# Order of table reads and weight loads in the state-space stage of a two-layer decoder trunk

## The chip, the cores and the metric

The kernel runs on one core of a Trainium2 chip. The metric is device time in microseconds (us) of one execution; the figure given is the median of the runs. Engines are called by their short names in the profile: PE is the matrix engine (TensorE), ACT is ScalarE, DVE is VectorE, POOL is GpSimd and SP is SyncE. All numbers are float32.

## The reference

Two layers work on a sequence of 512 tokens with 1024 channels. Layer 0 mixes tokens with a grouped complex state-space model (S5), layer 1 with attention; each is followed by a gated feed-forward part with a short convolution. Before each of the four parts there is an RMS norm, modulated by a shift and a scale that come from a conditioning vector c; the result is gated by a third vector of the same origin and added to the residual.

```python
def adaln_params(c, w, b):
    mod = jax.nn.silu(c) @ w + b
    shift, scale, gate = jnp.split(mod, 3, axis=-1)

def s5_mixer(h, w_in, ...):
    u = h @ w_in
    # 64 groups of 16 channels; each group drives 64 complex states:
    # x[t] = lb * x[t-1] + bb @ u[t];   y[t] = Re(c @ x[t])
    y = y + d_skip * u
    y = jax.nn.gelu(y)
    y = y * jax.nn.sigmoid(y @ w_glu)
    return y @ w_out
```

The change lies in the S5 part alone.

## The kernel before

The S5 part works on eight blocks of 128 channels (eight groups each). Tokens are cut into 64 places of 8 tokens. For one block m the work is:

1. **Projection.** u[m] = x @ w_in[m]: eight matmuls (`project`, L1270), evicted by ACT to the tile `uf` and written by SP to a DRAM scratch `s_ud` (`projected`, L1275 and L1276). SP reads it back in another layout, channel and token along the partitions (`read_u`, L1280; tile `u`). The read waits for the write to land.
2. **Kernel table.** Small matmuls (`s5_inputs`, L1032) make `w1` and the tile `kt`. DVE adds the skip weights `dd` to `kt`, and SP writes it to a DRAM scratch `s_z` (`s5_kernel`, L1047 and L1050). SP then reads it back as a Toeplitz table `tw`, 512 KB in rows of 512 bytes that overlap in DRAM (`s5_toeplitz`, L1057). The read waits for the write to land. ACT masks the table to `t` (`s5_masked`, L1066).
3. **States.** PE forms the state inputs of each place from `u` and `w1` (`s5_blocks`, L1090); DVE rotates, scans and rotates back (`s5_scan`, from L1106).
4. **Outputs.** PE adds what comes from the inputs of the place, `t` times `u` (`s5_from_inputs`, L1131), and what comes from the states (`s5_from_states`, L1142). ACT applies gelu, SP writes the result to scratch `s_yd` (`s5_gelu`, L1155 and L1156) and reads it back as `h` (L1159).

The loop `for m in range(KT - 2)` (L1347) pipelines this by hand. Round m runs the states and outputs of block m, the kernel table of block m+1 and the projection of block m+2. All engines run in the order in which the program is written (`manual_schedule`), and each engine takes its instructions, DMA issues among them, strictly in that order: an instruction that waits holds up all behind it on the same engine.

Two queues issue transfers here. SP issues the scratch writes and reads named above. POOL issues the loads from the inputs, since `self.loads` is set to POOL at L1318: the projection matrices `w_in` (`load_w`, 512 KB each, "raw<-in_s_w_in"), the skip weights (`load_d`, 64 KB each, "dd<-in_s_dd") and the modulation matrices ("raw<-in_ada_w", 512 KB each). These last belong to two generators: `ada` makes the gate of the S5 part out of eight matrices, and `ada2` shift and scale of the next part out of sixteen. Each `next(...)` of them runs the matmuls of two matrices (L226) and issues two further loads; the first `next` only issues four loads. A load waits until a slot of its tile is free: the tag `raw` has three slots, `w_hi` and `w_lo` five each.

Before the loop POOL carries out two small additions into a tile `gate`, whose value is used nowhere. The first (L1317) reads a parameter; the second (L1341) reads the first kernel table, so that the POOL instructions behind it are not issued until that table has landed. Behind it come the first four loads of `ada`. In round 0, POOL then issues the fourth projection matrix and the third skip weights (L1349 and L1350), and after round 0's outputs the last four loads of `ada`. SP reads in round 0 first the third u (L1368) and then the second kernel table (L1369).

## Time and profile before

| what | value |
|---|---|
| median of 3 runs | 1211.98 us (1211.89 to 1212.69) |
| profiled execution, its own time | 1213.4 us |
| its span, first to last instruction | 1211.6 us |
| mean granted PE clock | 0.992 |
| PE busy | 1178.7 us, 97% of the span |
| DVE busy | 1008.2 us, 83% |
| ACT busy | 614.7 us, 51% |
| POOL busy | 120.6 us, 10% |
| DMA moved | 182.00 MB, mean 150 GB/s |

Times in the rows are us from the start of the span. A row of a timeline has the start, the length, engine, source line, operation, output tile, input tile and count, and in square brackets how long the engine was idle before it and what ended that idle time. A row that starts a DMA on SP or POOL shows its issue; when the data landed is told by the DMA view, as us from issue to landing. Queue q1 carries what SP issues and q0 what POOL issues.

### The profile page before, as it was taken

The page shows a single profiled execution, that of the slowest core. Times are in us where ns is not written, and L with a number is a line of the kernel's source. Part 1 is how long each engine was busy: PE and PEld are TensorE (multiplying, and loading weights), DVE is VectorE, ACT ScalarE, POOL GpSimd, SP SyncE. Part 2 cuts the span into 40 slices and gives each one's busy share as a digit, 9 for nine tenths or more (in the row PEclk, how much of TensorE's full clock was granted, in tenths as well). Part 3 has the DMA queues.
Part 4 walks back from the last instruction along what each step waited for, and adds up shares of the span by engine and source line. Part 5 has one row for each costly group of instructions (what it writes and reads, how often), then busy time and mean ns, then how long its engine had stood idle before and what let it go on. Part 6 is the DMA issues. An engine that isn't in the chain of part 4 may idle for free.

```text
span 1211.6 us, 20653 instructions
## 1 busy us (share of the span) xinstructions
PE 1178.7 (97%) x7925; PEld 1019.7 (84%) x7925; DVE 1008.2 (83%) x1843; ACT 614.7 (51%) x1179; POOL 120.6 (10%) x227
## 2 busy tenths in 40 slices
PE   7979999999999999999999999999999999999997
PEld 2555678898989889999899888878989999999987
DVE  8967896879999999898698578876899888888865
ACT  3625563436445455555443566664366545545553
POOL 3211111100000000000000334430000000000000
PEclk9989999999999999999999999999999999999999
DMA  9596767832355555433445443432223332323331
GB/s 369 174 344 199 243 205 260 278 115 67 111 178 166 169 162 166 149 111 103 126 139 194 168 164 127 148 118 90 77 64 103 121 110 93 106 99 109 109 101 70
DMA packets 71826, 182.00 MB, mean 150 GB/s; under 512 B 23103, under 2 KB 24479, under 8 KB 70703
## 3 DMA queue, kind: packets, MB, share of 16 engines
q1 hardware_dynamic: 58767, 137.94, 35.2%
q0 software_dynamic: 11632, 41.95, 10.2%
q8 instruction: 62, 1.02, 0.3%
q10 hardware_dynamic: 1328, 0.79, 0.2%
q14 instruction: 37, 0.30, 0.1%
HBM read 173.73 MB, written 6.92 MB: 149 GB/s over the span
## 4 chain that ended last, share of the span: by engine, by line
PE 56%; issue 17%; DVE 6%; DMA 4%; ACT 1%; POOL 1%; SPq 0%; DVEq 0%; POOLq 0%; ACTq 0%
PE mmp L317 27%; PE mmp L586 16%; PE aux L586 6%; PE mmp L1594 2%; DVE w_lo L301 2%; PE aux L1733 1%; DMA raw<-in_s_w_out 1%; PE aux L1753 1%; DVE ada_raw L270 1%; PE aux L1703 1%; DMA ada_raw<-in_ada_t 1%; POOL ada_raw L256 1%; ACT w_hi L300 1%; DMA nf<-nfd 1%; DMA raw<-in_w_down 1%
## 5 line engine op out<-in xcount | busy, mean ns | idle before, releaser
L301 DVE TENSOR_TENSOR w_lo<-raw,w_hi 128x1024 fp32r<-128x1024 f32 (+4 forms) x173 | 182.8, 1061 | 26.7 <-ACT w_hi L300 26.2
L300 ACT ACTIVATE w_hi<-raw 128x1024 fp32r<-128x1024 f32 (+4 forms) x173 | 153.8, 899 | 89.6 <-PE mmp L317 34.5
L317 PE MATMUL mmp<-ghi,w_lo 128*128 128x512 f32 (+1 forms) x412 | 147.5, 358 | 1.1 <-DVE w_lo L301 1.1
L317 PE MATMUL mmp<-ghi,w_hi 128*128 128x512 f32 (+1 forms) x412 | 147.9, 359 | 0.3 <-DVE h L399 0.3
L317 PE MATMUL mmp<-glo,w_hi 128*128 128x512 f32 (+1 forms) x412 | 147.4, 358 | 0.0
L586 PE MATMUL mmp<-w_hi 128*128 128x256 f32 x420 | 116.6, 278 | 1.7 <-ACT nm_h L593 1.1
L317 PE MATMUL mmp<-a_hi,w_hi 128*128 128x512 f32 (+1 forms) x320 | 116.7, 368 | 1.5 <-ACT a_hi L469 1.5
L586 PE MATMUL mmp<-w_lo,w_hi 128*128 128x256 f32 x420 | 116.2, 277 | 0.0
L586 PE MATMUL mmp<-w_hi,w_lo 128*128 128x256 f32 x420 | 116.0, 277 | 0.0
L317 PE MATMUL mmp<-a_hi,w_lo 128*128 128x512 f32 (+1 forms) x320 | 114.4, 358 | 0.0
L317 PE MATMUL mmp<-a_lo,w_hi 128*128 128x512 f32 (+1 forms) x320 | 114.2, 358 | 0.0
L301 DVE TENSOR_TENSOR w_lo<-sums,w_hi 128x1024 fp32r<-128x1024 f32 x78 | 94.8, 1218 | 0.0
L300 ACT ACTIVATE w_hi<-sums 128x1024 fp32r<-128x1024 f32 x78 | 81.0, 1054 | 25.9 <-DVE sums L554 22.4
L593 ACT ACTIVATE nm_h<-mmp 128x256 f32<-128x256 f32 x105 | 39.3, 380 | 100.7 <-PE mmp L586 100.5
L317 PEld LDWEIGHTS mmp<-ghi,w_lo 128*128 128x128 f32 x412 | 77.4, 188 | 13.4 <-DVE w_lo L301 1.9
L317 PEld LDWEIGHTS mmp<-ghi,w_hi 128*128 128x128 f32 x412 | 77.4, 188 | 11.2 <-issue 0.4
L317 PEld LDWEIGHTS mmp<-glo,w_hi 128*128 128x128 f32 x412 | 77.4, 188 | 10.2
L586 PEld LDWEIGHTS mmp<-w_hi 128*128 128x128 f32 x420 | 78.9, 188 | 2.6 <-ACT nm_h L593 1.5
L586 PE MATMUL mmp<-a_hi,w_lo 128*128 128x256 f32 x280 | 77.8, 278 | 1.3 <-DVE w_lo L301 1.1
L586 PEld LDWEIGHTS mmp<-w_hi,w_lo 128*128 128x128 f32 x420 | 78.7, 188 | 0.2 <-DVE w_lo L301 0.2
L586 PEld LDWEIGHTS mmp<-w_lo,w_hi 128*128 128x128 f32 x420 | 78.9, 188 | 0.0
L586 PE MATMUL mmp<-a_hi,w_hi 128*128 128x256 f32 x280 | 77.9, 278 | 0.2 <-ACT w_hi L300 0.2
(335 smaller groups left out, 3123.3 us busy)
## 6 DMA issues: line engine op xcount, KB each, us to landing
raw<-in_w_up SPq DMA_DIRECT2D x88, 512.0 KB, 3.8
ada_raw<-in_ada_t POOLq DMA_DIRECT2D x40, 512.0 KB, 4.1
raw<-in_ada_w POOLq DMA_DIRECT2D x24, 512.0 KB, 6.2
nf<-nfd SPq DMA_DIRECT2D x8, 1152.0 KB, 6.5
raw<-in_ada_w SPq DMA_DIRECT2D x16, 512.0 KB, 9.9
raw<-in_fox_qk SPq DMA_DIRECT2D x16, 512.0 KB, 3.5
raw<-in_w_down SPq DMA_DIRECT2D x24, 320.0 KB, 3.0
rawd<-in_w_down SPq DMA_DIRECT2D x24, 256.0 KB, 3.2
```

Of the source, the lines that this page charges most:

```text
L256: (nc.gpsimd if late else nc.sync).dma_start(ws[n], src)
L270: nc.vector.tensor_tensor_reduce(w, w, self.c_row, 1.0, 0.0, ALU.mult, ALU.add, sums[:, j:j + 1])
L300: self.rounded = nc.scalar.activation(hi, src, AF.Copy).ins
L301: return nc.vector.tensor_tensor(lo, src, hi.bitcast(F32), ALU.subtract)
L317: self.last_mm = self.nc.tensor.matmul(o if len(xt.shape) == 2 else by_place(o), wt, xt, start=(k == 0 and n == 0), stop=(k == nk - 1 and ...
L586: self.last_mm = nc.tensor.matmul(o, wt[:, k], xt[:, k], start=(first and k == 0 and n == 0), stop=(k == H - 1 and n == 2), skip_group_che ...
L593: a = nc.scalar.activation(t, o, AF.Copy)
L1594: self.last_mm = nc.tensor.matmul(ps[q, b][:, :n], xt[:, k, tb], wt, start=(k == 0 and i == 0), stop=(k == KT - 1 and i == 2),)
L1703: nc.tensor.matmul(ps[b][r], q[i][a, tq], kk[j][a, :N], start=(n == 0), stop=(n == 2), tile_position=(64 * r, 0), skip_group_check=True,)
L1733: nc.tensor.transpose(pt[:, r - rs[0], k, :], s[:, r, k * P:(k + 1) * P], self.ident)
L1753: nc.tensor.matmul(pv[:, c * P:], self.v[:, hp, k, r].rearrange("p t d -> p (t d)"), pp[:, r, c + 3 * k:NB + 3 * k, :].rearrange("p b t -> ...
```

## The change

Three things are done, all in the S5 part:

- The fourth projection matrix (`load_w(3)`) and the third skip weights (`load_d(2)`) are issued by POOL ahead of the loop, right behind the second skip weights and ahead of the gate on the first kernel table, instead of in round 0. The rounds from 1 on are as before.
- In round 0, SP's read of the second kernel table (`s5_toeplitz(1)`) stands ahead of its read of the third u (`read_u(2)`). In the other rounds the order is as before.
- In round 0, POOL carries out one more addition into `gate`, which reads the second kernel table. Behind it in POOL's order come the last four loads of `ada` and all that POOL issues from round 1 on.

```diff
@@ -1319,6 +1319,8 @@
                 load_d(0)
                 load_w(2)
                 load_d(1)
+                load_w(3)
+                load_d(2)
                 read_u(0)
                 turns = self.s5_rotations(0)
                 next(turns)
@@ -1345,9 +1347,10 @@
                 turns = self.s5_rotations(2)
                 next(turns)
                 for m in range(KT - 2):
-                    if m + 3 < KT:
+                    if m and m + 3 < KT:
                         load_w(m + 3)
-                    load_d(m + 2)
+                    if m:
+                        load_d(m + 2)
                     ps = self.s5_blocks(ws[m], us[m])
                     if m:
                         self.s5_gelu(m - 1, yps.pop(m - 1))
@@ -1364,9 +1367,10 @@
                     if m:
                         next(turns)
                         t = self.s5_masked(tws.pop(m))
-                    else:
+                    tws[m + 1] = self.s5_toeplitz(m + 1)
+                    if not m:
+                        nc.gpsimd.tensor_tensor(gate, tws[1][:, 0, 0, 0:1], tws[1][:, 0, 0, 1:2], ALU.add)
                         read_u(m + 2)
-                    tws[m + 1] = self.s5_toeplitz(m + 1)
                     if m:
                         self.s5_read_y(m - 1)
                         run(steps[:4])
```

## The prediction

> **What bounds the kernel now.** I began with the page: TensorE (PE) is busy for nearly all of the span, so what can be won are stretches where it waits or runs at a lower clock.

> ```profile
> span 1211.6 us, 20653 instructions
> PE 1178.7 (97%) x7925; PEld 1019.7 (84%) x7925; DVE 1008.2 (83%) x1843; ACT 614.7 (51%) x1179; POOL 120.6 (10%) x227
> ```

> The edited loop makes one round for each channel block. The view of busy time by stretch, cut where PE begins each round's state matmuls (L1090), compares rounds m=1, 2 and 3 (columns: stretch, length, then each engine's busy us, PE clock, DMA share, GB/s); two short stretches follow from the same view.

> ```profile
> 66.57:93.33 26.76, 21.17 (x130) 13.72 (x129) 15.01 (x18) 5.51 (x19) 4.25 (x9) 0.75 0.83 303
> 93.33:111.55 18.22, 17.48 (x143) 11.70 (x139) 14.26 (x20) 11.37 (x37) 1.54 (x3) 0.99 0.60 177
> 111.55:127.39 15.84, 15.84 (x133) 10.38 (x129) 14.27 (x17) 8.71 (x28) 3.72 (x8) 1.00 0.90 295
> 80.00:84.00 4.00, 1.46 (x7) 1.46 (x8) 2.32 (x2) 3.42 (x11) 0.00 (x0) 0.51 1.05 393
> 88.00:92.00 4.00, 4.00 (x30) 2.23 (x32) 0.00 (x0) 0.00 (x0) 0.00 (x0) 0.50 0.29 66
> ```

> Round 3 is PE from end to end: 15.84 us busy, no idle, full clock. Round 1 issues the same matmuls to within some records (130 against 133) and takes 26.76 us: 5.59 us idle (26.76 less 21.17), and 21.17 us busy at a mean clock of 0.75, 5.33 us more than 15.84. The PE, ScalarE (ACT) and VectorE (DVE) timelines name the place.

> ```profile
> 65.58 1.05 PE L226 MATMUL mmp<-raw,s_sc 128*32 128x512 f32 x4 [0.99 <-DMA raw<-in_ada_w]
> 66.57 1.15 PE L1090 MATMUL aux<-u,w 128*64 128x64 f32 x32
> 69.93 7.03 PE L1270 MATMUL mmp<-a_x,raw 128*128 128x512 f32 x16
> 82.54 3.68 PE L1131 MATMUL aux<-u,t 128*128 128x64 f32 x16 [5.59 <-ACT t L1066]
> 89.76 3.64 PE L226 MATMUL mmp<-raw,s_sc 128*32 128x512 f32 x16
> 105.94 1.90 PE L1131 MATMUL aux<-u,t 128*128 128x64 f32 x16
> 79.92 2.57 ACT L1066 ACTIVATE t<-tw,first 128x128 f32<-128x128 f32 x8 [9.29 <-DMA tw<-s_z]
> 81.13 1.23 DVE L1004 TENSOR_TENSOR w<-w,x 128x1024 f32<-128x1024 f32 x1
> 94.71 0.69 DVE L1106 TENSOR_TENSOR m<-aux,rot 128x512 f32<-128x512 f32 x1 [12.36 <-PE aux L1090]
> ```

> After the projection (L1270, done at 76.96) PE needs t, which ACT masks from the second kernel table tw. ACT waits 9.29 us, from 70.63, until the table lands at 79.92; PE goes on at 82.54 with the clock halved, and the 16 L1131 matmuls take 3.68 us against 1.90 a round later. DVE then idles 12.36 us behind PE. So the end is set by one late transfer. Why it is late: rows of SyncE's queue (SP), then of GpSimd (POOL), then of the DMA view for 66 to 70, 77 to 79.5 and 46 to 56 us (a queue's packets, MB and share of the 16 DMA engines; for a transfer, last, the us to landing).

> ```profile
> 60.26 0.32 SPq L1050 DMA_DIRECT2D s_z<-kt  x1
> 65.37 0.37 SPq L1280 DMA_DIRECT2D u<-s_ud  x1
> 66.81 0.32 SPq L1057 DMA_DIRECT2D tw<-s_z  x1
> 73.39 2.52 SPq L1050 DMA_DIRECT2D s_z<-kt  x1
> 81.09 0.32 SPq L1057 DMA_DIRECT2D tw<-s_z  x1
> ```

> ```profile
> 35.65 0.54 POOL L1284 DMA_DIRECT2D dd<-in_s_dd  x1
> 55.38 0.47 POOL L1341 TENSOR_TENSOR s_gate<-tw 128x1 f32<-128x1 f32 x1 [19.20 <-DMA tw<-s_z]
> 56.23 2.12 POOL L194 DMA_DIRECT2D raw<-in_ada_w  x4 [0.38 <-issue]
> 58.34 0.54 POOL L194 DMA_DIRECT2D raw<-in_s_w_in  x1
> 58.86 0.55 POOL L1284 DMA_DIRECT2D dd<-in_s_dd  x1
> 59.39 1.06 POOL L194 DMA_DIRECT2D raw<-in_ada_w  x2
> ```

> ```profile
> q0 software_dynamic: 457, 1.65, 100.6%
> q1 hardware_dynamic: 77, 0.02, 2.1%
> tw<-s_z SPq DMA_DIRECT2D x1, 512.0 KB, 13.1
> ```

> ```profile
> q1 hardware_dynamic: 1303, 0.81, 102.2%
> q0 software_dynamic: 28, 0.10, 11.4%
> ```

> ```profile
> tw<-s_z SPq DMA_DIRECT2D x1, 512.0 KB, 3.5
> ```

> From 66 to 70 POOL's queue q0 moves 457 packets at full share, SP's queue q1 only 77. From 77 q0 has run dry and q1 takes everything. So the table read issued at 66.81 stands behind POOL's 512 KB loads and needs 13.1 us; the first table's read, with q0 empty, needed 3.5. Note also that the table's issue at 66.81 came 1.07 us after the u read's had ended (65.74): SP was waiting for the s_z write of 60.26.

> **The change part by part.** More rows are needed here: of the DMA view, the landing of one s_z write with q0 quiet (100 to 112), of modulation loads (56 to 62 and 60.1 to 60.6), of the third table (81 to 83) and of the first u (40 to 44); and the first u's issue and first use.

> ```profile
> s_z<-kt SPq DMA_DIRECT2D x1, 64.0 KB, 1.6
> raw<-in_ada_w POOLq DMA_DIRECT2D x6, 512.0 KB, 6.7
> raw<-in_ada_w POOLq DMA_DIRECT2D x1, 512.0 KB, 9.6
> tw<-s_z SPq DMA_DIRECT2D x1, 512.0 KB, 5.7
> u<-s_ud SPq DMA_DIRECT2D x1, 256.0 KB, 2.7
> ```

> ```profile
> 42.18 0.37 SPq L1280 DMA_DIRECT2D u<-s_ud  x1
> 48.15 1.15 PE L1090 MATMUL aux<-u,w 128*64 128x64 f32 x32
> ```

> (1) *Table read ahead of the third u.* By the row just named this alone wins nothing: the table cannot be issued before s_z has landed. It costs the u read the wait for s_z, some 1.4 us (65.37 to 66.81); that u is needed only when round 2 starts. Price 0; without that cover 1.4.
> (2) *The new gate.* A one-column addition that reads the second table; POOL, in order, stops at it. Behind it wait eight 512 KB loads and one dd: four modulation loads, the fifth projection matrix, three loads of the next modulation. In front remain only the four loads of 56.23, which drain first in either kernel. The s_z write then lands between 1.6 us (with q0 quiet) and 6.55 (60.26 to 66.81) after issue, so the table is issued at 61.9 to 66.8; with 3.5 us it lands at 65.4 to 70.3, and I take 68.5, near the upper end, because the four loads drain only about 64 to 65 (PE's wait for their last one ended at 65.58). PE needs t at 76.96, so the table by 76.96 - 2.57 = 74.4. Even the upper bound leaves 4.1 us. Hence the 5.59 us idle goes, and with it the half-clock stretch: 5.59 + 5.33 = 10.92 us, round 1 taking 15.84.

> On that half-clock stretch: the two rows at 80 and 88 show 0.51 and 0.50, and the clock stays low from PE's return at 82.54 until round 2, over 10 us of busy PE. [...]

> (3) *The deferred loads.* POOL resumes 0.85 us after the table lands (as 55.38 to 56.23): 66.3 to 71.2. Four loads at 0.53 us each are issued by 68.4 to 73.3 and land 6.7 to 9.6 us after issue, the last by 75.1 to 82.9. Their matmuls (L226) come in round 1 about 66.57 + 15.84 - 1.8 = 80.6 (half of the slow 3.64), the second half of them at 81.5. I take 0; the bound is a wait of 1.4.
> (4) *Fourth projection matrix and third dd sooner.* Two issues, 0.54 + 0.55 us, move from 58.34 to about 36.2, into the 19.20 us in which POOL waits for the first gate. What they meet is the first u: SP reads it at 42.18 and it lands 2.7 us later, at 44.9, while PE's first state matmuls start at 48.15. 0.52 MB at the 393 GB/s of the 80 us row is 1.3 us, under that slack of 3.2. Price 0; if uncovered, 1.3.

> (5) *A small term.* PE's 0.99 us wait at 65.58 is for a load that stays ahead of the gate: 0 to 0.99 may go; I take 0.

> *What is late next.* Round 2 would start at 66.57 + 15.84 = 82.41 on PE. DVE's last work of round 1 ends at 82.36, so DVE gives no new wait above some tenths. Round 2's own table: its s_z write is issued at about 73.4, and in the kernel before s_z and table together took from 73.39 to 86.8 (81.09 plus 5.7), 13.4 us. PE needs it at 82.41 + 12.61 (93.33 to 105.94) - 2.57 = 92.4, so 19.0 us are allowed. Round 3 is all PE and the span is 97% PE, so I carry the gain to the end undiminished.

> **Sum:** 5.59 idle + 5.33 half clock = 10.9 gained, all other terms 0. The profiled execution took 1213.4 us, 1.8 outside its span; less 10.9 it is 1202.5. The median shown, 1211.98, lies 1.4 under that execution; less 10.9 it is **1201.1**. With the bounds: 10.9 + 1.0 at best (1200.1), 10.9 - 1.4 - 1.4 - 1.3 with every cover gone (1205.2).

> **The rivals.**

> *B, the jam moves one round on.* The eight deferred loads (4.3 MB with the dd, 10.8 us at 393 GB/s) plus the six that follow when slots come free (3.1 MB, 8.0 us) now fill 70 to about 89 us, when SP moves round 2's s_z, table, ud and u. If s_z and table together need 19 to 24.7 us, PE waits up to 5.7 us in round 2 and, in the longer cases, loses the clock again (5.3). About half the gain stays: 1203 to 1210, say 1206. For it: q1's 77 packets in 4 us. Against it: that pair took 13.4 us with q0 just as full when it began. [...]

> *C, slower: strict precedence of q0.* Round 2's s_z lands only once q0 runs dry at 89, and the table, caught by the next loads, again needs 13.1: 102.1, t at 104.7 against 95.0, so 9.7 us idle and 5.3 at half clock, 15.0 lost against 10.9 won: 1216.1. It turns slower where the pair needs more than 24.7 us (5.6 idle plus 5.3). For it: q1 took everything only after q0 was dry. Against it: q1 never stood quite still, and POOL pauses for free slots.

> *D, it does not do what it says.* The table stays near 80 because its 512-byte pieces are slow by themselves or s_z lands late anyway: about 1212, no change. Against it: 3.5 us for the first table.

> **How the numbers follow.** Forecast 0.69 (1199 to 1205), B 0.17, D 0.08, C 0.06. Within 0.2% (2.4 us, about what a measurement of this kernel can tell from no change) are D and the longest waits of B. Faster 0.85, same 0.09, slower 0.06. Faster is the forecast and nearly all of B, slower is C. Range 1198.5 to 1207.5: it takes in the bounds, a little under the best for the run-to-run spread, and over half of B; C, D and the rest of B are left out.

> **What would show it.** The round from the second L1090 to the third at 15.8 to 16.5 us with clock 1.00; no idle before round 1's L1131; the second table landing 3 to 5 us after issue, before 71; POOL's second gate waiting some 8 to 11 us for it; DVE's wait before round 2's scan down from 12.36 to about 1. Wrong would be: a new wait of L1131 or L226 in rounds 1 and 2, a clock under 1 between 80 and 110, or SP's second table still needing over 8 us.

## The result

The changed kernel takes 1206.97 us, median of 5 runs (1203.91 to 1208.49), against 1212.69 us (1211.89 to 1215.73) for the kernel before beside it: a ratio of 0.9943, 95% interval 0.9922 to 0.9965. It is faster; the forecast was 1201.1, the range 1198.5 to 1207.5. Two later sets of runs of the same kernel gave 1203.3 and 1204.44 (ratios 0.9912 and 0.9931, below). Over all 18 runs its median is 1204.5, over all 66 runs of the kernel before 1213.2. So the gain is 8.7 us where 10.9 were forecast, and the first five runs lay at the slow end.

The profiled execution of the changed kernel took 1208.49 us. Its page begins:

```profile
span 1206.7 us, 20655 instructions
PE 1178.1 (98%) x7925; PEld 1019.4 (84%) x7925; DVE 1009.1 (84%) x1843; ACT 614.8 (51%) x1179; POOL 122.9 (10%) x228
```

The span is 4.9 us shorter. The view of busy time by stretch, cut again where PE begins the state matmuls (L1090) of rounds 0, 1 and 2, says where (columns as in the prediction; the last two rows are short stretches for the clock):

```profile
49.91:69.62 19.71, 19.17 (x130) 11.95 (x129) 18.06 (x24) 11.29 (x37) 2.32 (x5) 0.84 0.56 174
69.62:85.72 16.10, 16.10 (x132) 10.64 (x128) 14.27 (x17) 5.53 (x19) 7.50 (x15) 0.98 0.96 341
85.72:104.26 18.54, 17.33 (x143) 11.52 (x139) 14.27 (x20) 11.44 (x37) 1.61 (x4) 1.00 0.85 308
65.00:66.00 1.00, 1.00 (x12) 0.93 (x10) 1.00 (x2) 0.00 (x0) 0.00 (x0) 0.50 1.04 420
425.00:429.00 4.00, 3.93 (x10) 3.11 (x11) 2.89 (x4) 0.47 (x2) 0.00 (x0) 0.57 0.82 277
```

Round 1 went from 26.76 to 16.10 us, with PE busy throughout: 10.66 us won, 10.92 forecast. What the span does not show of it went elsewhere. This execution reached its first L1090 1.76 us later (49.91 against 48.15). The delay is there before any changed line runs: ACT's L833 starts at 35.86 against 34.12, and the first changed issue is POOL's at 36.13. Later executions lie between, before_again at 48.73 and after_third at 48.24. Still, four of the five profiles of kernels with the early loads reach that point at 49.3 or later and the eight others by 48.9, so that it is chance is likely, and not shown. Round 0 took 19.71 us instead of 18.42, because its clock was at half from 63.4 to 70.2 us. Round 2 took 0.32 us more. The remaining 2.4 us came later in the span, where one more stretch ran at half clock (the row of 425).

Now the steps of the round. PE's and ACT's rows, and then SP's and POOL's:

```profile
73.25 7.03 PE L1270 MATMUL mmp<-a_x,raw 128*128 128x512 f32 x16
73.80 2.56 ACT L1066 ACTIVATE t<-tw,first 128x128 f32<-128x128 f32 x8
80.11 1.89 PE L1131 MATMUL aux<-u,t 128*128 128x64 f32 x16
83.87 1.92 PE L226 MATMUL mmp<-raw,s_sc 128*32 128x512 f32 x16
86.92 0.69 DVE L1106 TENSOR_TENSOR m<-aux,rot 128x512 f32<-128x512 f32 x1 [1.25 <-PE aux L1090]
88.82 1.90 PE L1032 MATMUL aux<-s_both,x 128*128 128x160 f32 x12 [1.21 <-ACT yg L1155]
```

```profile
62.19 0.32 SPq L1050 DMA_DIRECT2D s_z<-kt  x1
67.86 0.32 SPq L1057 DMA_DIRECT2D tw<-s_z  x1
76.72 0.33 SPq L1050 DMA_DIRECT2D s_z<-kt  x1
82.47 0.33 SPq L1057 DMA_DIRECT2D tw<-s_z  x1
72.34 0.19 POOL L1372 TENSOR_TENSOR s_gate<-tw 128x1 f32<-128x1 f32 x1 [12.16 <-DMA tw<-s_z]
```

PE goes from the projection into L1131 without a wait, ACT's masking no longer waits for the table, DVE's 12.36 us behind PE have become 1.25, and L226, whose loads now leave POOL only after 72.34, does not wait either. The table lands 4.3 us after its issue (13.1 before).

### The profile page after: what moved, and what is told of

Read it like the earlier page. It is cut to its first block, busy times and chain, and to the rows that moved or that the text cites. A ratio compares the mean times of both kernels' runs of the same rounds, so it can differ in the third digit from the quotient of the medians.

```text
span 1206.7 us, 20655 instructions
## 1 busy us (share of the span) xinstructions
PE 1178.1 (98%) x7925; PEld 1019.4 (84%) x7925; DVE 1009.1 (84%) x1843; ACT 614.8 (51%) x1179; POOL 122.9 (10%) x228
## 3 DMA queue, kind: packets, MB, share of 16 engines
q0 software_dynamic: 11632, 41.95, 10.2%
## 4 chain that ended last, share of the span: by engine, by line
PE 52%; DVE 21%; DMA 7%; issue 4%; ACT 2%; DVEq 0%; ACTq 0%; SPq 0%
PE mmp L317 31%; PE mmp L586 8%; DVE w_lo L301 7%; PE aux L586 3%; DMA rawd<-in_w_down 3%; DMA raw<-in_w_up 2%; DVE sums L554 2%; DVE conv L638 2%; DVE h L399 2%; DVE nm_t L554 2%; PE aux L1757 2%; PE mmp L1312 2%; PE aux L1737 2%; PE mmp L1598 2%; DVE ada_raw L270 1%
## 5 line engine op out<-in xcount | busy, mean ns | idle before, releaser
L586 PEld LDWEIGHTS mmp<-w_hi 128*128 128x128 f32 x420 | 78.8, 188 | 2.7 <-ACT w_hi L300 1.4
L399 DVE SCALAR_TENSOR_TENSOR h<-mmp,par,h 128x512 f32<-128x512 f32 (+1 forms) x104 | 68.7, 663 | 14.4 <-PE mmp L317 14.3
L586 PEld LDWEIGHTS mmp<-w_lo,w_hi 128*128 128x128 f32 x420 | 78.9, 188 | 0.0
## 6 DMA issues: line engine op xcount, KB each, us to landing
raw<-in_w_up SPq DMA_DIRECT2D x88, 512.0 KB, 4.0
ada_raw<-in_ada_t POOLq DMA_DIRECT2D x40, 512.0 KB, 4.1
raw<-in_ada_w POOLq DMA_DIRECT2D x24, 512.0 KB, 6.7
raw<-in_ada_w SPq DMA_DIRECT2D x16, 512.0 KB, 9.2
raw<-in_fox_qk SPq DMA_DIRECT2D x16, 512.0 KB, 3.5
rawd<-in_w_down SPq DMA_DIRECT2D x24, 256.0 KB, 3.2
```

The costliest lines, as they stand in the source:

```text
L399: add = self.nc.vector.scalar_tensor_tensor(h, ps, self.par[i][:, 16 + m:17 + m], h, op0=ALU.mult, op1=ALU.add,)
L586: self.last_mm = nc.tensor.matmul(o, wt[:, k], xt[:, k], start=(first and k == 0 and n == 0), stop=(k == H - 1 and n == 2), skip_group_che ...
```

## The experiments

The prediction held that the gate carries the gain and that the new order on SP carries none. The theories have these names in the expectations: **loads** (GpSimd's 512 KB loads in flight make the table late; this is the prediction's own), **order** (the table was late because it stood behind u on SP's queue), **early** (the fourth projection matrix was the transfer in the way), **either** (order and gate each suffice), and in u_on_act **turns** against **load**. All runs are of one core; each ratio is against runs of the kernel before on the same chip: 1213.21 us median of 17 for swap_only, early_only, gate_swap and after_again, 1214.78 of 11 for gate_early and the three gs runs, 1213.02 of 16 for before_again and after_third, and 1212.89 of 7 for u_on_act.

### Only SP's order (swap_only)

```diff
-                    else:
-                        read_u(m + 2)
                     tws[m + 1] = self.s5_toeplitz(m + 1)
+                    if not m:
+                        read_u(m + 2)
```

> Of the three edits only the new order on SP is kept: the second table's read ahead of the third u's; no second gate, fourth projection matrix and third dd loaded in round 0 as before. Theory 'loads' (what makes the second table late is GpSimd's 512 KB loads in flight around it): the table is still issued when s_z has landed, 60.3 + some 6.5 = about 67, still needs about 13 us, and TensorE still idles 4 to 6 us before round 1's L1131 and then runs at half clock; time within 0.2% of the kernel before (1212). Rival 'order' (the table was late because it stood behind u on SP's queue): it lands 3 to 5 us after issue, the idle time goes and the time falls by 5 us or more.

Measured: 1203.82 us (1200.24 to 1206.23, 6 runs), ratio 0.9911, interval 0.9889 to 0.9933. One moved line gives the whole gain, as "order" had it, though the table does not land in the 3 to 5 us that "order" expected. SP's, ACT's and PE's rows:

```profile
66.60 0.32 SPq L1057 DMA_DIRECT2D tw<-s_z  x1
67.01 0.39 SPq L1280 DMA_DIRECT2D u<-s_ud  x1
73.99 2.58 ACT L1066 ACTIVATE t<-tw,first 128x128 f32<-128x128 f32 x8 [3.62 <-DMA tw<-s_z]
76.62 2.00 PE L1131 MATMUL aux<-u,t 128*128 128x64 f32 x16
```

The prediction was right that the table is not issued any sooner: 66.60 here, 66.81 before. But it lands 7.4 us after issue instead of 13.1. The next view is of the DMA queues, for the kernel before from 72 to 73 us and for this one from 71 to 72 (packets, MB, share of the 16 engines), each with the landing of one transfer:

```profile
q0 software_dynamic: 123, 0.38, 94.1%
q1 hardware_dynamic: 122, 0.03, 13.7%
...
u<-s_ud SPq DMA_DIRECT2D x1, 256.0 KB, 13.4
```

```profile
q1 hardware_dynamic: 54, 0.22, 53.7%
q0 software_dynamic: 54, 0.19, 47.1%
...
u<-s_ud SPq DMA_DIRECT2D x1, 256.0 KB, 11.9
```

The two queues move the same number of packets. SP's 122 packets carry 0.03 MB, 256 bytes each (that is u); its 54 carry 0.22 MB, some 4 KB each (that is the table). The access patterns fit this: for one partition the table's eight rows of 512 bytes lie one behind the other in s_z, while u's eight rows of 256 bytes lie 32 KB apart in s_ud. If the engines take one packet of each queue in turn, as 122 against 123 and 54 against 54 suggest, u's 1024 packets (256 KB of 256 bytes) need some ten microseconds at about 100 a microsecond, and a table behind them waits as long; the table itself is only about 128 packets. In the kernel before it did wait so: from 70 to 76 us q1 moved 624 packets with 0.16 MB and q0 627 with 2.24 MB, and only from 77 to 78 us did q1 carry the bytes of a table (172 packets, 0.38 MB). By then q0 was running dry (10 packets in that microsecond). In this kernel u, now second and issued 1.64 us later, lands at 78.9 (67.01 plus 11.9), where before it landed at 78.8 (65.37 plus 13.4): the exchange cost u nothing.

The table is in time by very little: t is ready at 76.57 and PE needs it at 76.62.

### Only the early loads (early_only)

```diff
                 load_d(1)
+                load_w(3)
+                load_d(2)
...
-                    if m + 3 < KT:
+                    if m and m + 3 < KT:
                         load_w(m + 3)
-                    load_d(m + 2)
+                    if m:
+                        load_d(m + 2)
```

> Of the three edits only the earlier loads are kept: the fourth projection matrix and the third dd go out behind the second dd; no second gate, old order on SP. Theory 'loads': 0.59 MB of the some 6.5 MB that GpSimd issues from 56 to 69 are gone, at about 0.4 MB/us worth 1.4 us; the second table lands 1 to 2 us sooner and TensorE's idle time falls from 5.6 to about 4, the half clock stays: time 0 to 3 us under the kernel before. Rival 'early' (the projection matrix was the transfer in the way): the idle time and the half clock go, 8 us or more. The first u must land before TensorE's first state matmuls in either case (no idle time before round 0's L1090).

Measured: 1211.56 us (1203.33 to 1215.44, 12 runs), ratio 0.9967, interval 0.9941 to 0.9992.

```profile
67.68 0.32 SPq L1057 DMA_DIRECT2D tw<-s_z  x1
78.66 2.56 ACT L1066 ACTIVATE t<-tw,first 128x128 f32<-128x128 f32 x8 [7.56 <-DMA tw<-s_z]
81.28 3.68 PE L1131 MATMUL aux<-u,t 128*128 128x64 f32 x16 [3.85 <-ACT t L1066]
```

The loads in the way are 0.59 MB fewer, and PE's wait falls from 5.59 to 3.85 us, as "loads" expected; "early" falls. A second profile of the kernel before (before_again, below) has 4.81, so the early loads are worth 1 to 1.7 us of wait. The half clock behind it stays (3.68 us for L1131, a mean clock of 0.75 from 66.82 to 92.07 us), so round 1 still takes 25.25 us. Three of the twelve runs (1203.33, 1204.13, 1206.16) had a mean clock of 0.997 or more where the slower ones, from 1212 us on, had 0.991 to 0.994. Either the wait was shorter in those three or it passed without the loss of the clock; none of them was profiled, so this is open. The kernel before, too, has two runs so short among its 66 (1204.92 and 1205.81).

### Gate and order, without the early loads (gate_swap)

```diff
-                    else:
-                        read_u(m + 2)
                     tws[m + 1] = self.s5_toeplitz(m + 1)
+                    if not m:
+                        nc.gpsimd.tensor_tensor(gate, tws[1][:, 0, 0, 0:1], tws[1][:, 0, 0, 1:2], ALU.add)
+                        read_u(m + 2)
```

> The second gate and the new order on SP are kept, the fourth projection matrix and the third dd are loaded in round 0 as before, ahead of the gate. Theory 'loads': five 512 KB loads instead of four stand ahead of the gate, s_z and the table land some 1.4 us later than in the changed kernel, which its slack (TensorE needs the table about 5 us after it landed) covers; round 1 lasts about 16 us, time within 0.2% of the changed kernel. Rival 'early': it falls back towards the kernel before by 3 us or more.

Measured: 1202.6 us (1200.22 to 1206.23, 6 runs), ratio 0.9902, interval 0.9878 to 0.9926. Queues from 66 to 70 us, and ACT's wait:

```profile
q1 hardware_dynamic: 298, 0.55, 48.9%
q0 software_dynamic: 7, 0.01, 0.6%
...
tw<-s_z SPq DMA_DIRECT2D x1, 512.0 KB, 3.9
```

```profile
71.01 2.58 ACT L1066 ACTIVATE t<-tw,first 128x128 f32<-128x128 f32 x8 [0.53 <-DMA tw<-s_z]
```

The gate does what the prediction said: q0 is all but empty and the table takes 3.9 us. The early loads are not needed for the gain.

### The changed kernel again (after_again)

No edit.

> The changed kernel once more, unedited. In its first profile round 1 won 10.7 us as forecast, but 1.8 us were lost before the changed lines, 1.3 us in round 0, where the clock stood at 0.5 for 6.8 us, and 2.4 us later, round a 3.4 us stretch at half clock at 425 us. Theory 'chance': these three are not tied to the change; here they fall elsewhere or are missing, round 1 again lasts 16 to 16.5 us, and the span varies by some us between runs of either kernel. Rival 'cause': the change brings the low clock in round 0 about, and it is there again at the same place, with round 0 lasting about 19.7 us.

Measured: 1203.3 us (1202.36 to 1205.82, 6 runs), ratio 0.9912, interval 0.9892 to 0.9932. Round 1 took 16.37 us, and round 0 again ran at half clock from 63.5 us on for 6.8 us. In this group the changed kernel, gate_swap and swap_only cannot be told apart.

### Only gate and early loads, u ahead of the table (gate_early)

The changed kernel with SP's two reads in the old order:

```diff
+                    if not m:
+                        read_u(m + 2)
                     tws[m + 1] = self.s5_toeplitz(m + 1)
                     if not m:
                         nc.gpsimd.tensor_tensor(gate, tws[1][:, 0, 0, 0:1], tws[1][:, 0, 0, 1:2], ALU.add)
-                        read_u(m + 2)
```

> The second gate and the early loads are kept, the new order on SP is undone: SP reads the third u ahead of the second table. New theory 'either': the table was late because on SP's own queue it stood behind the u read's 1024 packets of 256 bytes while GpSimd's loads took nearly all of the DMA; it is enough either to put the table first or to keep GpSimd's loads away. Here the loads are kept away: u and table land within 4 to 6 us of issue one after the other, round 1 lasts about 16 us, time as the changed kernel (1203 to 1207). Rival 'order alone': the table needs to stand first, gate or no gate; it lands 8 us or more after issue, and TensorE waits before round 1's L1131 as before (1210 or more).

Measured: 1204.87 us (1199.92 to 1209.63, 6 runs), ratio 0.9919, interval 0.9891 to 0.9947.

```profile
72.02 2.58 ACT L1066 ACTIVATE t<-tw,first 128x128 f32<-128x128 f32 x8 [0.58 <-DMA tw<-s_z]
77.61 1.90 PE L1131 MATMUL aux<-u,t 128*128 128x64 f32 x16
```

```profile
q1 hardware_dynamic: 1117, 0.55, 55.8%
...
tw<-s_z SPq DMA_DIRECT2D x1, 512.0 KB, 5.0
u<-s_ud SPq DMA_DIRECT2D x1, 256.0 KB, 2.8
```

With q0 empty (it has no row from 66 to 70 us), u's 1024 packets wait for nobody: u lands in 2.8 us, and the table behind it in 5.0. So either edit suffices. They remove the same wait, and their gains do not add.

### The third u on another queue (u_on_act)

What swap_only showed was still one pair of transfers in another order. Here the order of the program is that of the kernel before, but ACT's queue reads that u:

```diff
-            def read_u(m):
+            def read_u(m, queue=nc.sync):
...
-                nc.sync.dma_start(us[m], ud[m].rearrange("g c j b -> (c j) g b"))
+                queue.dma_start(us[m], ud[m].rearrange("g c j b -> (c j) g b"))
...
                     else:
-                        read_u(m + 2)
+                        read_u(m + 2, nc.scalar)
```

> The kernel before with one transfer on another queue: the third u is read by ACT's queue instead of SP's, at the same place in the program; table, gate and loads as before. Two theories of why the table is late beside GpSimd's loads. 'Turns': the DMA engines take one packet of each queue in turn, whatever its size, and within SP's queue the u read's 1024 packets of 256 B stood ahead of the table's. Then the table is now first in its queue and lands 6.5 to 8.5 us after issue (some 3.4 us until its first packet, as in the kernel with the table ahead, and about 128 packets of 4 KB at 35 to 55 a microsecond); no idle above 1 us before round 1's L1131, no low clock behind it, round 1 17 to 18 us, the three rounds 51.5 to 54.5 us, median 1202 to 1206. In the stretch 70 to 76 us each queue that is not empty shows about the same number of packets. 'Load': what is late is late because GpSimd's queue is full, and its place among SP's transfers is not the point. Then the table still needs 11 to 13 us, PE idles 4 to 6 us, and the median stays at 1211 to 1214.

Measured: 1205.32 us (1204.26 to 1206.62, 4 runs), ratio 0.9939, interval 0.9917 to 0.9962. Queues from 72 to 73 us (q10 is ACT's), the landing, and ACT's and PE's rows:

```profile
q0 software_dynamic: 52, 0.20, 48.9%
q1 hardware_dynamic: 52, 0.19, 47.0%
q10 hardware_dynamic: 52, 0.01, 5.8%
```

```profile
tw<-s_z SPq DMA_DIRECT2D x1, 512.0 KB, 6.8
```

```profile
73.70 2.57 ACT L1066 ACTIVATE t<-tw,first 128x128 f32<-128x128 f32 x8 [2.43 <-DMA tw<-s_z]
77.44 1.89 PE L1131 MATMUL aux<-u,t 128*128 128x64 f32 x16
```

52 packets of each of three queues in one microsecond, carrying 0.20, 0.19 and 0.01 MB. The table, first in its queue, lands in 6.8 us although the u was issued before it (64.70 against 66.92) and q0 is as full as ever. "Turns" is borne out, "load" falls. A third queue moved no more bytes, 0.40 MB in the microsecond here and 0.41 before; but the table no longer stands behind u's packets, and here that is worth the whole wait, 5.59 us in before.

### What is next in the way (gs_gelu, gs_split, gs_split_gelu)

Three tries for more, on gate_swap. gs_gelu issues block 1's gelu right after its outputs, for the 1.21 us that PE waits in round 2; gs_split puts round 0's table matmuls (L1032) between the halves of the projection, for the waits of round 0; the third does both.

```diff
 gs_gelu
-                    if m:
+                    if m and m != 2:
                         self.s5_gelu(m - 1, yps.pop(m - 1))
...
                         if m == 1:
+                            self.s5_gelu(m, yps.pop(m))
 gs_split
                     if not m:
-                        run(steps)
+                        run(steps[:4])
+                    inputs(m + 1)
+                    if not m:
+                        run(steps[4:])
...
-                    inputs(m + 1)
```

> Second gate and new order on SP, late loads (as the run with gate and order), and the gelu of block 1 is issued right after its outputs in round 1 instead of after round 2's state matmuls. In the profiles with the gate TensorE waits 1.21 us in round 2 for that gelu on ScalarE, which holds the last two PSUM buffers. Expected: that wait goes or shrinks under 0.3, round 2 falls from 18.5 to about 17.3 us, time 1 us under the run with gate and order (about 1201.6). Rival: the wait passes to VectorE's reading of the state inputs (0.74 us in the profiles without the gate) and only 0.5 us are won.

> Second gate and new order on SP, late loads, and in round 0 the small table matmuls (L1032) stand between the two halves of the projection (L1270) instead of behind it, so TensorE's small matmuls come less in one stretch. [...]

> Both of the two foregoing edits on top of gate and order: round 0 at 18 us, round 1 at 16, round 2 at 17.3; about 1.5 us under the run with gate and order, 1201 in the median, the fastest runs below 1199.5. If the two edits do not add up, the one that fails shows by its round.

Measured: 1203.44 us (1201.51 to 1210.64), 1203.55 (1201.48 to 1206.11) and 1203.35 (1201.52 to 1208.75), 6 runs each; ratios 0.9919 (0.9895 to 0.9943), 0.9914 (0.9895 to 0.9933) and 0.992 (0.9897 to 0.9942). None beats gate_swap (ratio 0.9902), where gs_gelu was expected to gain 1 us and gs_split_gelu 1.5; but the intervals are some 5 us wide, so the times cannot settle gains of that size. With gs_gelu, round 2 takes 17.57 us instead of 18.54 (about 17.3 expected), and the median does not show it. With gs_split, round 0 falls to 15.90 us, and round 1 gets a new wait, on DVE:

```profile
69.27 0.78 PE L1032 MATMUL aux<-s_both,x 128*128 128x160 f32 x4 [1.59 <-DVE m L1107]
```

Round 1 then takes 17.67 us, and the two rounds together no less than in the unedited kernels below. In the profile of gs_split_gelu PE came to round 3 12.2 us sooner than in that of before (99.37 against 111.55). In the last rounds it lost 10.2 of them: it reached L165 at 191.34 against 193.28, after a wait for t and 13.7 us at half clock (mean clock 0.62 from 164 to 182 us):

```profile
165.27 3.25 PE L1131 MATMUL aux<-u,t 128*128 128x64 f32 x16 [3.08 <-ACT t L1066]
```

### Both kernels once more (before_again, after_third)

Both profiles of the changed kernel had the half clock in round 0, and none of the others had it. One more profile of each kernel, without an edit, was to tell whether it belongs to the change.

> The kernel before, unedited, profiled a second time, to see which of its stretches belong to the kernel and which to one execution. Both theories of round 1 (order, gate) rest on the same wait: PE should again idle 5 to 6 us before round 1's L1131, the second table should again take 12 to 14 us from issue to landing, and about 13.7 us at half clock should follow; the round 26 to 27.5 us. If the late table or the half clock belonged to that one execution, the round takes under 24 us. The instruction before any changed line that starts the first L1270 of round 0 may lie 1 to 4 us away from the 38.93 us of the first profile (theory 'start by chance'), or within 0.3 us of it (the later start belongs to the changed kernel). Median within 0.2% of the other runs of before.

> The changed kernel, unedited, profiled a third time, for one open point: the 6.8 us at half clock from 63.4 us on, in round 0, which both profiles of it show and none of the others. Theory 'chance of the clock's windows': this profile may have it or not; if it has not, round 0 (first L1090 to second) takes 18.2 to 18.6 us instead of 19.7 and the span is about 1.3 us shorter from there on. Theory 'belongs to the kernel': the stretch is there a third time, starting within 1 us of 63.4 less any difference in the start. Both expect round 1 at 15.8 to 16.4 us without idle time before L1131, and a median of 1202 to 1208.

Measured: before_again 1213.56 us (1209.09 to 1216.1, 10 runs), ratio 0.9999, interval 0.9973 to 1.0026; after_third 1204.44 us (1202.1 to 1205.54, 7 runs), ratio 0.9931, interval 0.9908 to 0.9955. In before_again PE idled 4.81 us before round 1's L1131 (5 to 6 expected), the table took 12.4 us from its issue, the half clock lasted 10.2 us (13.7 expected), and round 1 took 26.89, as expected; so the late table belongs to the kernel.

```profile
81.69 3.68 PE L1131 MATMUL aux<-u,t 128*128 128x64 f32 x16 [4.81 <-ACT t L1066]
```

Rounds 0 and 1 of before_again, and then of after_third:

```profile
48.73:65.05 16.32, 16.32 (x130) 10.49 (x129) 15.26 (x22) 12.00 (x37) 5.90 (x11) 1.00 0.71 242
65.05:91.94 26.89, 20.87 (x130) 13.74 (x128) 17.00 (x20) 5.51 (x19) 5.32 (x11) 0.81 0.86 309
```

```profile
48.24:64.17 15.93, 15.93 (x129) 10.45 (x128) 14.89 (x22) 11.93 (x37) 2.65 (x5) 1.00 0.62 209
64.17:81.81 17.64, 16.07 (x130) 10.39 (x128) 17.30 (x20) 5.53 (x19) 7.53 (x15) 1.00 0.92 326
```

Round 0 of after_third runs at full clock, so the half clock there is no fixed part of the change. Its round 1, though, is 17.64 us (15.8 to 16.4 expected), with 1.57 us idle: the same wait on DVE as in gs_split.

```profile
68.72 0.78 PE L1032 MATMUL aux<-s_both,x 128*128 128x160 f32 x4 [1.56 <-DVE m L1107]
```

The kernel before has this wait too when its round 0 is short: 1.21 us in before_again. Over rounds 0 and 1 DVE is busy 14.89 + 17.30 = 32.19 of 33.57 us in after_third: with the table in time, it is the next limit. The rounds of all profiles, each from the times at which PE starts L1090:

| kernel | round 0 | round 1 | round 2 | together |
|---|---|---|---|---|
| before | 18.42 | 26.76 | 18.22 | 63.40 |
| before_again | 16.32 | 26.89 | 18.05 | 61.26 |
| early_only | 17.51 | 25.25 | 18.52 | 61.28 |
| after | 19.71 | 16.10 | 18.54 | 54.35 |
| after_again | 19.25 | 16.37 | 18.54 | 54.16 |
| after_third | 15.93 | 17.64 | 18.54 | 52.11 |
| swap_only | 16.48 | 17.29 | 18.05 | 51.82 |
| u_on_act | 16.81 | 17.51 | 18.05 | 52.37 |
| gate_early | 18.04 | 15.83 | 18.54 | 52.41 |
| gate_swap | 18.54 | 15.84 | 18.54 | 52.92 |
| gs_gelu | 19.14 | 15.83 | 17.57 | 52.54 |
| gs_split | 15.90 | 17.67 | 18.54 | 52.11 |
| gs_split_gelu | 16.19 | 17.39 | 17.56 | 51.14 |

Where the table is in time, a short round 0 goes with a longer round 1: what is not waited for in the one is waited for, behind DVE, in the other. The last column is therefore the one to compare.

## Why the prediction was right, and where not

**The size and the place.** Right. The idle 5.59 us went, and the half clock with it; round 1 gave 10.66 us in the first pair of profiles (forecast 10.92), and 10.1 as a mean over both profiles of before (26.83) and the three of the changed kernel (16.70). The half-clock term was read off rows, and so it came out: in both profiles of before the clock stayed low for some 10 us of busy PE behind the wait, and where the wait is gone from round 1 its clock is full but for the tail of round 0's low stretch. Part of this is luck: the prediction put the whole gain down to the gate, and by swap_only the new order would have won as much had the gate done nothing. And the first median, 1206.97, lay only half a microsecond inside the range.

**Part (1), "alone wins nothing": wrong, and the step that failed.** I priced the exchange by the time of issue, which indeed did not move (66.81 before, 66.60 in swap_only). What moved was the table's place in SP's queue, behind or ahead of 1024 packets that take their turns with q0's. The row "q1 hardware_dynamic: 77" I read as a queue starved of bytes by a full one. By the microsecond, from 66 to 70 us, q1 moved 8, 0, 0 and 69 packets: first a late start, which no run explains (last section), and then the small packets, 0.02 MB in 77, at a pace that drew level with q0's from 70 us on (624 packets against 627 by 76 us). I had the 0.02 MB beside the 77 and did not divide.

**Part (2), the gate.** It works as described: table landing 4.3 us after issue (forecast 3 to 5), q0 all but empty meanwhile (15 packets from 66 to 70 us). But the gain does not hang on it: gate_early, without the new order, and swap_only, without the gate, each give it. Beside the order, the gate buys margin: t is ready at 76.36 in the changed kernel, 3.75 us before PE's L1131 at 80.11, against 0.05 in swap_only. No run here shows that margin as time. Two sizes were off. The table was issued at 67.86 where I gave 61.9 to 66.8 (of that, 1.76 us is the later start): the s_z write ahead of it still took 5.67 us from issue to the table's issue, 3.59 in after_third. And the gate waited 12.16 us, not 8 to 11.

**Parts (3) and (4), the deferred and the early loads.** Priced at 0; L226 does not wait in round 1, nor L1090 in round 0. The bound of 1.3 us in part (4) left out the dd: 0.59 MB at the same rate are 1.5 us, still under its slack of 3.2. early_only shows what the early loads are worth without the other edits: 1 to 1.7 us of wait.

**Part (5), PE's 0.99 us wait in round 0.** 0 was taken, and it is not a term of the change: it is absent in the three profiles of the changed kernel and in before_again, but 0.95 us in gate_swap and 1.16 in gate_early, which have the gate.

**What is late next.** "No new wait above some tenths" from DVE was too low: 1.56 us in round 1 of after_third, and in round 2 PE waits 1.21 us for ACT's yg where it waited 0.74 for DVE. Round 2 is 0.4 us longer for it (18.54 against a mean of 18.14).

**From 10.9 to 8.7.** With the means of the profiles: round 1 wins 10.1, round 0 loses 0.9 (18.30 against 17.37; two of the three had the half clock), round 2 loses 0.4. That leaves 8.8 over the three rounds, and the medians differ by 8.7. That they agree so well is partly chance: the spans of these five profiles differ by only 6.2 us in the mean (1209.9 against 1203.7), since those of the changed kernel started 0.9 us later and lost 1.7 more behind round 2. What the rounds do show is that the forecast was too high by assuming that the other rounds stay as they are, on one execution whose three rounds (63.40) were 2.1 us longer than those of the second profile. The first five runs showed 5.7 us; after_again and after_third, each against the kernel before on its chip, gave 9.9 and 8.6.

**The rivals.** B (jam in round 2) and C (strict precedence of q0) fell. Round 2's s_z was issued at 76.72 and its table at 82.47, and the table landed 6.4 us later: 12.2 us for the pair, of the 19.0 allowed, with q0 as full as B had supposed (873 packets, 3.12 MB from 82 to 92 us). Neither ACT nor PE waited for it. C's ground, that q1 moves freely only when q0 is dry, is refuted by 54 packets against 54 in swap_only. D (no effect) fell with the 4.3 us. The rival that held, that SP's order alone does it, was not in the list.

**Not settled:** why the changed kernel had the half clock in round 0 in two profiles of three when the ten profiles of the other kernels show none there. Where it was present PE had waited 0.54 and 0.36 us for kt just before, but gate_swap (0.33) and gs_gelu (0.81) had such a wait too.

## What to carry to other kernels

Price a moved transfer by what stands ahead of it in its queue, counted in packets, and not by when it is issued: in these runs each packet beside a full queue cost one turn, whether it carried 256 bytes or 4 KB (122 packets beside 123 of q0's in before, 54 beside 54 in swap_only). Read the queue rows by the microsecond, and divide bytes by packets, before calling a queue starved; a small-packet transfer should follow the urgent one, or go to another queue: here the table then landed 7.4 and 6.8 us after its issue instead of 13.1. When one change holds several edits, run each alone: here two of them removed the same wait, and a single moved line would have done, with less margin.

## What the runs showed of the hardware that was not expected

```profile
60.84 2.12 PE L1131 MATMUL aux<-u,t 128*128 128x64 f32 x16 [0.54 <-ACT kt L1041]
62.89 3.23 PE L1142 MATMUL aux<-ua,w 64*128 64x63 f32 x32
66.05 3.64 PE L226 MATMUL mmp<-raw,s_sc 128*32 128x512 f32 x16
```

The first packets of a read came late beside a full q0: in swap_only the table was issued at 66.60, and from 66 to 70 us q1 moved 2 packets, q0 460.

```profile
q0 software_dynamic: 460, 1.67, 102.4%
q1 hardware_dynamic: 2, 0.00, 0.0%
```

It is the same in the kernel before: u was issued at 65.37, and q1 moved no packet from 67 to 69. With q0 empty, in gate_early, u was issued at 66.54 and 301 packets moved from 67 to 68. The turns explain the rate after that, not this delay of over 3 us, which stays open.
